# Stick-breaking attention weights by sigmoid and running product with queries on partitions, and one set of adaLN sums by ScalarE products and accumulating transfers

## The chip, the cores and the metric

The kernel runs on one core of one Trainium2 chip. The metric is the device time of one execution in microseconds, the median of several runs. A profiled execution of the kernel before took 1203.4 us; its span in the profile, from the first instruction to the last, is 1201.6 us, so 1.8 us lie around the span.

## The reference, cut to what matters

A trunk of two layers over 512 tokens of width 1024, batch 1. Layer 0 mixes tokens by stick-breaking attention (16 heads of 64), layer 1 by a gated token MLP; each is followed by a SwiGLU of width 2816, and every sub-layer takes a shift, a scale and a gate from a conditioning vector (adaLN). The two pieces that the change touches:

```python
def ada_modulation(c, w, b):
    m = jax.nn.silu(c) @ w + b
    shift, scale, gate = jnp.split(m, 3, axis=-1)
...
        before = s_idx < t_idx
        log_beta = jax.nn.log_sigmoid(z)
        log_1m = jnp.where(before, jax.nn.log_sigmoid(-z), 0.0)
        later = lax.cumsum(log_1m, axis=3, reverse=True) - log_1m
        a = jnp.where(before, jnp.exp(log_beta + later), 0.0)
        outs.append(jnp.einsum('bhts,bhsd->bhtd', a.astype(v.dtype), v[:, :, :kend]))
```

So the weight of key s for query t is sigmoid(z[t,s]) times the product of (1 - sigmoid(z[t,r])) over all keys r between s and t.

## The kernel before, in words

All matrix products are made of three float32r matmuls: each operand is split into a high part (a float32r copy) and a low part (the difference), and `mm3` adds high·high, high·low and low·high. `split` (L90) writes the high part on ScalarE (or on VectorE with `hi_dve`) and the low part on VectorE (L95).

The program goes through these stages: norm and transposes of x, V and the first Q and K (0 to 66 us of the span), the second half of V (to about 98 us), eight passes over pairs of heads (98 to 296 us; pair i holds heads 2i and 2i+1), the output projection, the first SwiGLU, the gated MLP, the second SwiGLU.

In the attention stage `pe["chain"]` ties TensorE to the order in which the code is written. The other engines' streams are put in order by the scheduler when the program is built, and each engine runs its own stream strictly in order. `filler()` is a generator of other TensorE work: for each later pair, 8 steps of three 512-column matmuls for Q and 8 for K, then the first steps of the output projection; `fill(n)` takes n steps, and `FILLS` says how many go between the parts of a pair, 16 a pair. The rest of a pair before the change:

- `scores(js)`: z of a set of key blocks, keys on partitions, queries along the free axis, for both heads. The sets are B31 (blocks 3 and 1, 512 columns), B2 (256) and B0 (512). A matmul with the constant `mask_r` adds a large negative number to masked places. Then softplus(z) by ScalarE (Abs L763, Exp L765, Ln L766) and VectorE (L767), split into `sp`.
- `weigh(js, h)`: matmuls with a constant triangle and a constant block of -1 subtract, from z in PSUM, the sums of softplus over the later keys; ScalarE takes Exp (L796), VectorE splits the weights into `ar`.
- `values(js, h)`: V times the weights, added up in one PSUM bank a head (`av`).
- `finish()`: splits the output into `o`.

`Bg("G0", "A0", "B0")` (L276, L519) is the background work of this stage: for gate, scale and shift of the first boundary it loads eight blocks of 128 x 1024 weights each through SyncE's queue into a pool of two buffers (`fwork["raw"]`), and VectorE adds block times silu(c) to a sum (`ada_stt`, L270). One `bg.step` does one block; `fill` makes one step after every third filler step. Afterwards ones-matmuls (`adaps`) add the sum over partitions.

The output projection's and the SwiGLUs' own `Bg` objects work the same way.

Of the kernel before, what the change touches and what calls it, by code (L numbers as in the profile page):

```python
# [8 lines left out]
F32 = mybir.dt.float32  # L9
# [4 lines left out]
P = 128  # L14
# [12 lines left out]
def trunk(ctx: ExitStack, tc: tile.TileContext, A: dict, out: bass.AP):  # L27
# [228 lines left out]
    cr = consts.tile([P, 5, P], F32R, name="cr")  # L256
    ident_r, tri_r, mask_r, ones_r, mones_r = [cr[:, i, :] for i in range(5)]
# [18 lines left out]
    class Bg:  # L276
# [5 lines left out]
        def __init__(self, *parts, slots=False):  # L282
            self.slots = slots

            self.parts = [
                (n, int(s), int(s) + (n != "G"), {"G": 2, "A": 1, "B": 0}[n]) for n, s in parts
            ]
            self.gen = self.run()

        def run(self):  # L290
            for name, at, s, part in self.parts:
                acc = slot(F32, name, 1, D)[:, 0, :]
                ada[name, at] = acc
                nc.gpsimd.memset(acc, 0.0)
                load(acc[0:1, :], A["adab"][s, part])
# [223 lines left out]
    bg = Bg("G0", "A0", "B0")  # L519
# [136 lines left out]
    cc = stp.tile([P, 5, P], F32, name="cc")  # L656
# [6 lines left out]
    with tc.tile_pool(name="att", bufs=1) as att, tc.tile_pool(name="att2", bufs=2) as att2:  # L663
# [46 lines left out]
        FILLS = (3, 0, 3, 0, 1, 1, 2, 2, 4, 0)  # L710
# [10 lines left out]

        def attend(i):

            ob = []
            sps, zb = {}, {}
# [10 lines left out]
            def scores(js):  # L736
# [3 lines left out]
                zs = [bank(f"z{js[0]}h0"), bank(f"z{js[0]}h1")]  # L740
                zb[js] = zs
                for j in js:
                    o, n = offs[j], T - P * j
                    ks = slice(j * P, (j + 1) * P)
# [9 lines left out]
                if len(js) == 2:  # L754
                    nd = 2 * P
                    m = cr[:, 2:3, :].to_broadcast([P, 2, P])
                for h in range(2):
                    mm(zs[h][:, :nd], ident_r, m, False, False)
                t = npool.tile([P, 2, 512], F32, tag="n", name=nm("t"))
                for h in range(2):  # L760
                    z = zs[h]
                    tn = t[:, h, :N]
                    act.activation(tn, z[:, :N], AF.Abs)  # L763
                    with tc.issue_after(table.ins):
                        act.activation(tn, tn, AF.Exp, scale=-1.0)  # L765
                    act.activation(tn, tn, AF.Ln, bias=oneb[:])  # L766
                    dve.scalar_tensor_tensor(tn, z[:, :N], 0.0, tn, ALU.max, ALU.add)  # L767
                    sp = att.tile(
# [471 lines left out]
```

## Time and profile before

| | |
|---|---|
| runs | 1202.38, 1207.81, 1210.34 us; median 1207.81 us |
| profiled execution | 1203.4 us |
| its span | 1201.6 us |
| TensorE matmul busy | 1170.4 us, 97% of the span |
| VectorE / ScalarE / GpSimd busy | 885.1 us (74%) / 623.4 us (52%) / 18.2 us (2%) |
| granted TensorE clock | 0.999 |
| eight passes over the pairs | 98.2 to 296.4 us |

How to read it: matmuls overlap, so a TensorE that is busy throughout isn't one at its peak; the length of a stretch is better read from the starts of its matmuls. A row of groups gives the mean length of one instruction. The chain of waits follows the work that ended last back to its releasers. Idle time of an engine counts only where another one waits for it.

### The profile page before, as it was taken

The page shows a single profiled execution, that of the slowest core. Times are in us where ns is not written, and L with a number is a line of the kernel's source. Part 1 is how long each engine was busy: PE and PEld are TensorE (multiplying, and loading weights), DVE is VectorE, ACT ScalarE, POOL GpSimd, SP SyncE. Part 2 cuts the span into 40 slices and gives each one's busy share as a digit, 9 for nine tenths or more (in the row PEclk, how much of TensorE's full clock was granted, in tenths as well). Part 3 has the DMA queues.
Part 4 walks back from the last instruction along what each step waited for, and adds up shares of the span by engine and source line. Part 5 has one row for each costly group of instructions (what it writes and reads, how often), then busy time and mean ns, then how long its engine had stood idle before and what let it go on. Part 6 is the DMA issues. An engine that isn't in the chain of part 4 may idle for free.

```text
span 1201.6 us, 18615 instructions
## 1 busy us (share of the span) xinstructions
PE 1170.4 (97%) x7408; PEld 1029.0 (86%) x7408; DVE 885.1 (74%) x1221; ACT 623.4 (52%) x1071; POOL 18.2 (2%) x30
## 2 busy tenths in 40 slices
PE   6898999999999999999999999999999999999998
PEld 4676778787899999999887897898999999998886
DVE  4878887776698989887768766566988888783213
ACT  6455777787565555556224553535655555572212
POOL 0100000000000000000000000000000000000000
PEclk9999999999999999999999999999999999999999
DMA  8666342120443444335888466314424444245211
GB/s 316 240 208 208 110 152 78 36 71 18 140 158 107 146 138 144 131 126 171 263 278 269 158 198 223 104 73 140 135 94 155 127 155 127 89 125 173 89 53 70
DMA packets 48635, 174.15 MB, mean 145 GB/s; under 512 B 5658, under 2 KB 5786, under 8 KB 48548
## 3 DMA queue, kind: packets, MB, share of 16 engines
q1 hardware_dynamic: 46820, 166.67, 42.6%
q0 software_dynamic: 1728, 6.29, 1.4%
q8 instruction: 58, 0.95, 0.3%
q14 instruction: 29, 0.24, 0.1%
HBM read 164.56 MB, written 8.39 MB: 144 GB/s over the span
## 4 chain that ended last, share of the span: by engine, by line
PE 74%; DVE 10%; DMA 10%; ACT 3%; issue 3%; SPq 0%; DVEq 0%; ACTq 0%
PE r L71 31%; PE y L71 19%; DMA rawada<-in_ada 6%; PE pqk L71 4%; PE gu L71 4%; PE v L71 3%; PE av L71 2%; PE u L71 2%; DVE wl L95 2%; PE z3h L71 2%; PE z0h L71 2%; DVE B L270 1%; DVE A L270 1%; ACT wh L94 1%; PE tp L79 1%
## 5 line engine op out<-in xcount | busy, mean ns | idle before, releaser
L71 PE MATMUL y<-wh,as 128*128 128x512 f32 x832 | 263.9, 395 | 0.3 <-DVE G L328 0.3
L94 ACT ACTIVATE wh<-raw 128x1024 fp32r<-128x1024 f32 x112 | 118.3, 1059 | 200.8 <-PE y L71 100.8
L95 DVE TENSOR_TENSOR wl<-raw,wh 128x1024 fp32r<-128x1024 f32 x112 | 136.5, 1221 | 109.0 <-ACT wh L94 108.9
L71 PEld LDWEIGHTS y<-wh,as 128*128 128x128 f32 x832 | 156.2, 188 | 37.2 <-DVE G L328 0.8
L71 PE MATMUL r<-Sh,wl 128*128 128x256 f32 x608 | 170.3, 280 | 0.0
L71 PE MATMUL r<-Sh,wh 128*128 128x256 f32 x608 | 170.0, 280 | 0.0
L71 PE MATMUL r<-Sl,wh 128*128 128x256 f32 x608 | 170.0, 280 | 0.0
L71 PE MATMUL y<-wl,as 128*128 128x512 f32 x416 | 164.3, 395 | 0.0
L95 DVE TENSOR_TENSOR wl<-f,wh 128x1024 fp32r<-128x1024 f32 x76 | 92.7, 1220 | 36.4 <-ACT wh L94 36.4
L94 ACT ACTIVATE wh<-f 128x1024 fp32r<-128x1024 f32 x76 | 80.7, 1061 | 71.4 <-PE r L71 64.8
L71 PEld LDWEIGHTS r<-Sh,wh 128*128 128x128 f32 x608 | 114.6, 189 | 0.0
L71 PEld LDWEIGHTS r<-Sl,wh 128*128 128x128 f32 x608 | 114.5, 188 | 0.0
L71 PEld LDWEIGHTS r<-Sh,wl 128*128 128x128 f32 x608 | 114.5, 188 | 0.0
L71 PEld LDWEIGHTS y<-wl,as 128*128 128x128 f32 x416 | 78.2, 188 | 18.0
L71 PE MATMUL r<-hTh,wh 128*128 128x256 f32 x304 | 89.0, 293 | 0.0
L71 PE MATMUL r<-hTl,wh 128*128 128x256 f32 x304 | 84.9, 280 | 0.0
L71 PE MATMUL r<-hTh,wl 128*128 128x256 f32 x304 | 80.2, 280 | 0.0
L71 PEld LDWEIGHTS r<-hTh,wh 128*128 128x128 f32 x304 | 57.2, 188 | 5.3 <-DVE gu L963 1.0
L71 PE MATMUL r<-hTh,b 128*128 128x256 f32 x304 | 60.7, 282 | 0.0
L94 ACT ACTIVATE wh<-rawx 128x1024 fp32r<-128x1024 f32 x38 | 40.4, 1062 | 35.3 <-PE r L71 30.9
L71 PEld LDWEIGHTS r<-hTl,wh 128*128 128x128 f32 x304 | 57.3, 189 | 0.1
L71 PEld LDWEIGHTS r<-hTh,wl 128*128 128x128 f32 x304 | 55.2, 188 | 0.0
(245 smaller groups left out, 2658.7 us busy)
## 6 DMA issues: line engine op xcount, KB each, us to landing
rawada<-in_ada SPq DMA_DIRECT2D x80, 512.0 KB, 4.5
raw<-in_wdown SPq DMA_DIRECT2D x44, 512.0 KB, 4.1
rawy<-in_wy SPq DMA_DIRECT2D x38, 512.0 KB, 3.6
rawx<-in_wx SPq DMA_DIRECT2D x38, 512.0 KB, 4.3
raw<-in_wqk SPq DMA_DIRECT2D x16, 512.0 KB, 3.7
ada<-in_ada0p SPq DMA_DIRECT2D x12, 512.0 KB, 8.8
raw<-in_wgu SPq DMA_DIRECT2D x12, 512.0 KB, 4.0
xd<-x POOLq DMA_DIRECT2D x12, 512.0 KB, 2.9
```

The costliest lines, as they stand in the source:

```text
L71: b = nc.tensor.matmul(o, l, r, start=start, stop=stop, skip_group_check=True)
L79: last_tp[0] = nc.tensor.transpose(o, i, ident)
L94: act.activation(hi, src, AF.Copy)
L95: dve.tensor_tensor(lo, src, hi.bitcast(F32), ALU.subtract)
L270: dve.scalar_tensor_tensor(acc, w, sc[:, kk : kk + 1], acc, ALU.mult, ALU.add)
```

## The change

1. Time is reversed outside the kernel: x goes in with its tokens in reverse order, the output is reversed back, and the gated MLP's constants are turned to match. Causal order then runs along rising indices of the free axis.
2. `scores` swaps its operands: queries on partitions, keys along the free axis. ScalarE takes Sigmoid (`be`) of each head and then 1 - `be` for both heads at once (`ga`, L791). VectorE makes the running product of `ga` along the free axis (`left`, L798, one scan for each query block and head) and multiplies it by `be` (L801). The Abs/Exp/Ln, the softplus splits and the matmuls of `weigh` go.
3. The weights now have queries on partitions, and V needs keys there: `flip` transposes them on TensorE in blocks of 128 x 128 into a PSUM bank (`tw`) and splits that into `ar`, the high part now on ScalarE. `values` multiplies V by them.
4. The order of a pair and `FILLS` are new; a pair still holds 16 filler steps.
5. `Bg` of this stage adds up its 24 blocks in another way (`transfers`): GpSimd's queue loads a block into the same two buffers, ScalarE multiplies it in place by silu(c) (L305), and GpSimd's queue sends it on with an adding transfer into the sum in SBUF (L306). Gate, scale and shift go in turn. The 24 multiply-adds of VectorE go. The other `Bg` objects stay.

The diff, cut to its core:

```diff
+        def transfers(self):
+            accs = [self.begin(*p) for p in self.parts]
+            for k in range(KD):
+                for (name, at, s, part), acc in zip(self.parts, accs):
+                    raw = fwork["raw"].tile([P, D], F32, tag="raw2", name=nm("rawada"))
+                    nc.gpsimd.dma_start(out=raw[:], in_=A["ada"][s, part, k])
+                    yield
+                    act.activation(raw[:], raw[:], AF.Copy, scale=sc[:, k : k + 1])
+                    nc.gpsimd.dma_start(out=acc, in_=raw[:], accum_op=ALU.add)
...
-    bg = Bg("G0", "A0", "B0")
+    bg = Bg("G0", "A0", "B0", summed=True)
...
-        FILLS = (3, 0, 3, 0, 1, 1, 2, 2, 4, 0)
+        FILLS = (3, 2, 3, 2, 2, 2, 2)
...
                         mm3(
-                            zs[h][:, o : o + n], kt[r, 0, ks], kt[r, 1, ks],
-                            q[r, 0, j * P : T], q[r, 1, j * P : T], j == js[0], False,
+                            z[h][:, o : o + n], q[r, 0, js_], q[r, 1, js_],
+                            kt[r, 0, j * P : T], kt[r, 1, j * P : T],
+                            j == js[0], False,
                         )
...
+                b = att.tile([P, 2, T], F32, tag="be", bufs=2, name=nm("be"))
+                g = att.tile([P, 2, T], F32, tag="ga", bufs=3, name=nm("ga"))
+                with tc.issue_after(table.ins):
+                    for h in range(2):
+                        act.activation(b[:, h, :N], z[h], AF.Sigmoid)
+                last_act[0] = act.activation(g[:, :, :N], b[:, :, :N], AF.Copy, scale=-1.0, bias=1.0)
+                e = left[nleft[0] % 2]
+                nleft[0] += 1
                 for h in range(2):
...
+                    for j in js:
+                        o, n = offs[j], T - P * j
+                        gj = g[:, h, o : o + n]
+                        dve.tensor_tensor_scan(
+                            e[:, h, o + 1 : o + n + 1], gj, gj, 1.0, ALU.mult, ALU.bypass
+                        )
+                dve.tensor_tensor(g[:, :, :N], b[:, :, :N], e[:, :, :N], ALU.mult)
...
+            def flip(blocks, h):
+                ps = bank("tw")
+                n = 0
+                for jj, js in blocks:
+                    for j in js:
+                        g, o = weights[j]
+                        o += (jj - j) * P
+                        transpose(ps[:, n : n + P], g[:, h, o : o + P])
+                        n += P
+                ar = att2.tile([P, 2, T], F32R, tag="ar", name=nm("ar"))
+                split(ar[:, 0, :n], ar[:, 1, :n], ps[:, :n])
+                turned[blocks[0][0], h] = ar
...
+        LATE = ((2, (2,)), (3, (2, 3)))
+        EARLY = ((0, (0,)), (1, (0, 1))), ((2, (0, 1)), (3, (0, 1)))
...
             scores(B0)
             fill(next(F))
-            values(B2, 0)
-            values(B2, 1)
+            flip(LATE, 0)
+            flip(LATE, 1)
+            fill(next(F))
+            values(LATE, 0, False)
+            values(LATE, 1, False)
             fill(next(F))
             if i + 1 < NPAIR:
                 cur = attend(i + 1)
                 cur[0](B31)
             fill(next(F))
-            weigh(B0, 0)
-            weigh(B0, 1)
+            for h in range(2):
+                flip(EARLY[0], h)
             fill(next(F))
+            for h in range(2):
+                values(EARLY[0], h, False)
+                flip(EARLY[1], h)
+            fill(next(F))
+            for h in range(2):
+                values(EARLY[1], h, True)
+            finish()
             if i + 1 < NPAIR:
                 cur[0](B2)
             fill(next(F))
```

Three places show how the instruction streams change. A number behind a name counts tiles.

VectorE, middle of a pair. `t` is softplus, `sp` and `ar` are low halves of splits, `wl` and `k` those of a weight and of K. Before:

```order
L95 TENSOR_TENSOR k_1466<-pqk_1341,k_1466 128x512
L95 TENSOR_TENSOR wl_1603<-raw_1600,wh_1602 128x1024
L767 SCALAR_TENSOR_TENSOR t_1482<-z0h_269_1472,t_1482 128x512
L767 SCALAR_TENSOR_TENSOR t_1482<-z0h_270_1473,t_1482 128x512
L95 TENSOR_TENSOR sp0h_272_1487<-t_1482,sp0h_272_1487 128x512
L95 TENSOR_TENSOR sp0h_273_1494<-t_1482,sp0h_273_1494 128x512
```

And now, in pair 3, from the scans of set B0 (the first row) to the splits of the first early flip:

```order
L798 SCALAR_TENSOR_TENSOR left_585<-ga_1594 128x512 x2
L95 TENSOR_TENSOR ar_1618<-tw_1614,ar_1618 128x384
L801 TENSOR_TENSOR ga_1594<-be_1593,left_585 128x1024
L95 TENSOR_TENSOR ar_1625<-tw_1621,ar_1625 128x384
L95 TENSOR_TENSOR wl_1814<-raw_1811,wh_1813 128x1024
L95 TENSOR_TENSOR k_1662<-pqk_1569,k_1662 128x512
L798 SCALAR_TENSOR_TENSOR left_584<-ga_1692 128x128
L798 SCALAR_TENSOR_TENSOR left_584<-ga_1692 128x384
L798 SCALAR_TENSOR_TENSOR left_584<-ga_1692 128x128
L798 SCALAR_TENSOR_TENSOR left_584<-ga_1692 128x384
L95 TENSOR_TENSOR ar_1711<-tw_1707,ar_1711 128x384
L801 TENSOR_TENSOR ga_1692<-be_1691,left_584 128x1024
```

The low halves of the late flips (`ar_1618`, `ar_1625`) stand behind the scans of B0, the second one also behind B0's product with `be`; those of the first early flip stand behind the four scans of the next pair's B31.

TensorE, end of K of the next pair. Before, with the last matmul of K (`pqk_1341`) in the first row:

```order
L71 MATMUL pqk_1341<-hTh_130,wl_979 128x512
L71 MATMUL z0h_269_1472<-q_1074,k_1205 128x512 x3
L71 MATMUL z0h_270_1473<-q_1074,k_1205 128x512 x3
L71 MATMUL z0h_269_1472<-cr 128x128
L71 MATMUL z0h_270_1473<-cr 128x128
L71 MATMUL pqk_1497<-hTh_124,wh_1083 128x512
L71 MATMUL pqk_1497<-hTl_125,wh_1083 128x512
L71 MATMUL pqk_1497<-hTh_124,wl_1084 128x512
L71 MATMUL av_265_1449<-ar2h_263_1438,Vh_133 128x256 x2
L71 MATMUL av_265_1449<-ar2h_263_1438,Vl_137 128x256
L71 MATMUL av_266_1456<-ar2h_264_1446,Vh_133 128x256 x2
L71 MATMUL av_266_1456<-ar2h_264_1446,Vl_137 128x256
```

Behind these rows came two more filler steps and then the scores that read the new K. Now:

```order
L71 MATMUL pqk_1095<-hTh_130,wl_798 128x512
L71 MATMUL pqk_1183<-hTh_124,wh_857 128x512
L71 MATMUL pqk_1183<-hTl_125,wh_857 128x512
L71 MATMUL pqk_1183<-hTh_124,wl_858 128x512
L71 MATMUL z3h_233_1197<-k_1180,q_1088 128x128 x3
```

One filler step stands between the last matmul of K (`pqk_1095`) and the scores that read it (`k_1180`).

ScalarE in pair 1, where the products for adaLN (`rawada`) now stand; `be` and `ga` are sigmoid and its complement, `ar` high halves, `wh` a weight's, `k` K's:

```order
L790 ACTIVATE be_1115<-z0h_215_1105 128x512
L790 ACTIVATE be_1115<-z0h_216_1106 128x512
L305 ACTIVATE rawada_1158<-rawada_1158,sc 128x1024
L791 ACTIVATE ga_1116<-be_1115 128x1024
L94 ACTIVATE ar_1140<-tw_1136 128x384
L94 ACTIVATE ar_1147<-tw_1143 128x384
L305 ACTIVATE rawada_1195<-rawada_1195,sc 128x1024
L94 ACTIVATE wh_1335<-raw_1333 128x1024
L94 ACTIVATE k_1180<-pqk_1095 128x512
L305 ACTIVATE rawada_1248<-rawada_1248,sc 128x1024
L305 ACTIVATE rawada_1289<-rawada_1289,sc 128x1024
L790 ACTIVATE be_1213<-z3h_233_1197 128x512
```

GpSimd's queue, which held no instruction in this stage before, now alternates loads and adding transfers:

```order
L303 DMA rawada_866<-in_ada 128x1024
L303 DMA rawada_897<-in_ada 128x1024
L306 DMA G_673<-rawada_866 128x1024
L306 DMA A_676<-rawada_897 128x1024
L303 DMA rawada_938<-in_ada 128x1024
L303 DMA rawada_987<-in_ada 128x1024
L306 DMA B_679<-rawada_938 128x1024
L306 DMA G_673<-rawada_987 128x1024
```

Of the 24 products on ScalarE, six stand ahead of pair 0's sigmoids of B2, six more behind these in pair 0, seven in pair 1 and five in pair 2. A load waits until the adding transfer out of the same buffer is done, a product waits for its load, and everything behind the product on ScalarE waits with it.

More of the change, by code (lines that the diff above doesn't have):

```diff
@@ L719, in fill @@
                     bg.step(1)
+        left = [att.tile([P, 2, T + 4], F32, name=nm("left")) for _ in range(2)]
+        for t in left:
+            nc.gpsimd.memset(t[:], 1.0)
+        nleft = [0]
         def attend(i):
             ob = []
-            sps, zb = {}, {}
+            weights = {}
             vc = slice(i % 4 * P, (i % 4 + 1) * P)
@@ L801, in values @@
[L801 to L814 removed]
+                    mm(z[h][:, :nd], ident_r, m, False, False)
```

131 lines of the change are left out of this document (43 added, 88 removed).

## The prediction

> **What bounds the kernel now.** I read the page's first lines, then busy times by stretch, one stretch a pair of heads, then the chain of waits inside two pairs, then the groups of VectorE and ScalarE.
>
> ```profile
> span 1201.6 us, 18615 instructions
> ...
> PE 1170.4 (97%) x7408; PEld 1029.0 (86%) x7408; DVE 885.1 (74%) x1221; ACT 623.4 (52%) x1071; POOL 18.2 (2%) x30
> ```
>
> The columns of the next rows are length, then busy time (and instructions) of TensorE, its weight loads, VectorE, ScalarE, GpSimd, then granted clock, DMA share, GB/s.
>
> ```profile
> 98.20:126.70 28.50, 24.43 (x136) 19.10 (x135) 23.88 (x34) 17.48 (x34) 0.00 (x0) 1.00 0.58 185
> 126.70:151.40 24.70, 24.70 (x140) 19.69 (x139) 20.37 (x34) 18.05 (x36) 0.00 (x0) 1.00 0.37 109
> 151.40:177.40 26.00, 24.87 (x140) 19.68 (x139) 22.46 (x35) 17.96 (x36) 0.00 (x0) 1.00 0.49 159
> 177.40:201.80 24.40, 24.40 (x141) 19.97 (x140) 18.76 (x34) 19.06 (x38) 0.00 (x0) 1.00 0.21 65
> 201.80:229.40 27.60, 26.14 (x146) 20.81 (x145) 21.04 (x37) 20.36 (x41) 0.00 (x0) 1.00 0.17 58
> 229.40:254.50 25.10, 25.10 (x144) 20.51 (x144) 17.69 (x31) 20.14 (x40) 0.00 (x0) 1.00 0.14 43
> 254.50:278.30 23.80, 23.64 (x136) 19.21 (x135) 15.68 (x29) 17.04 (x35) 0.00 (x0) 1.00 0.26 89
> 278.30:296.40 18.10, 18.08 (x96) 13.86 (x95) 11.43 (x23) 11.94 (x22) 0.00 (x0) 1.00 0.00 0
> ```
>
> The full pairs take 24 to 28 us, and TensorE is busy nearly throughout at full clock (the first pair apart), while VectorE is idle for 4 to 8 us of each and ScalarE for 5 to 11. In this stage TensorE sets the time; other engines matter only when they make it wait. The chain says what its 24 us hold:
>
> ```profile
> 172.29 2.79 PE pqk L71 x12
> 175.08 0.93 PE z2h L71 x8
> 176.01 1.55 PE av L71 x6
> ...
> 179.66 1.84 PE z3h L71 x12
> ...
> 183.60 0.86 PE z2h L71 x8
> 184.46 1.78 PE av L71 x12
> ...
> 186.94 1.27 PE z0h L71 x8
> ...
> 188.94 0.72 PE av L71 x6
> ...
> 191.05 1.50 PE z3h L71 x14
> ...
> 194.40 2.56 PE z0h L71 x16
> ```
>
> A filler step is three of the `pqk` matmuls, 2.79 / 4 = 0.70 us, and 16 of them make 11.2. Scores with masks are 1.27 + 1.50 + 0.93 = 3.70, `weigh` is 1.84 + 0.86 + 2.56 = 5.26, `values` 1.78 + 0.72 + 1.55 = 4.05. Sum 24.2, against stretches of 24.4 and 24.7: before the change nearly nothing waits.
>
> **The change part by part: TensorE's work.** `weigh` goes: -5.26 us a pair. Scores keep their shapes. The transposes are 20 a pair (10 for each head):
>
> ```profile
> 344.81 1.09 PE L79 MATMUL tp<-identt,t 128*128 128x128 f32 x8 [0.34 <-DVE t L387]
> 345.65 0.37 PE L71 MATMUL gu<-hTl,wh 128*128 128x256 f32 x1
> ```
>
> Eight of the same type start within 345.65 - 344.81 = 0.84 us, 0.105 each, so +2.10. `values` keeps its columns but cuts them into twelve 128-wide and twenty-four 256-wide matmuls. The 256-wide cost 0.72 / 6 = 0.12 above, the 128-wide 0.10:
>
> ```profile
> 185.21 0.33 PE L71 MATMUL av<-ar3h,Vh 128*128 128x128 f32 x2
> 185.38 0.27 PE L71 MATMUL av<-ar3h,Vl 128*128 128x128 f32 x1
> 185.50 0.40 PE L71 MATMUL av<-ar3h,Vh 128*128 128x384 f32 x1
> ```
>
> (three between 185.21 and 185.50). That is 4.1 us, as before. TensorE's work falls by 3.15 us to 21.0 us a pair, 25 us in all. Were that the whole story, the time would be 1178.
>
> **New waits in a pair.** Here are the rows that price the new chain of ScalarE and VectorE.
>
> ```profile
> L95 DVE TENSOR_TENSOR wl<-raw,wh 128x1024 fp32r<-128x1024 f32 x27 | 33.0, 1221 | 13.1 <-ACT wh L94 13.1
> L95 DVE TENSOR_TENSOR ar3h<-a,ar3h 128x512 fp32r<-128x512 f32 x16 | 11.0, 690 | 0.4
> ...
> L767 DVE SCALAR_TENSOR_TENSOR t<-z0h,t 128x512 f32<-128x512 f32 x16 | 10.3, 687 | 7.8 <-ACT t L766 7.8
> ...
> L270 DVE SCALAR_TENSOR_TENSOR A<-rawada,sc,A 128x1024 f32<-128x1024 f32 x8 | 10.3, 1282 | 3.2 <-DMA rawada<-in_ada 3.2
> ...
> L95 DVE TENSOR_TENSOR ar2h<-a,ar2h 128x256 fp32r<-128x256 f32 x16 | 6.8, 425 | 0.5
> ```
>
> ```profile
> L94 ACT ACTIVATE wh<-raw 128x1024 fp32r<-128x1024 f32 x26 | 27.5, 1058 | 31.8 <-PE pqk L71 16.1 <-DMA raw<-in_wqk 4.5 <-PE y L71 4.2
> ...
> L763 ACT ACTIVATE t<-z0h 128x512 f32<-128x512 f32 x16 | 8.7, 596 | 3.0 <-PE z0h L71 3.0
> ```
>
> Sigmoid I price like the 512-wide ScalarE row (0.6, two in 1.1 us), the complement and each product for adaLN like the 1024-wide one (1.06), the product of `be` and `left` like `wl` (1.22), the low half of a 384-wide flip between 0.43 and 0.69, at 0.55. No row shows a scan. It can't be quicker than a plain pass over 512 columns, 0.69 us; and since each column needs the product of the one before, which none of these rows does, I take two passes, the time of 1024 plain columns less a little, 1.2 us (upper end 1.28). [...]
>
> Now I walk through an undisturbed pair, from the start of its scores of B0, with 0.1 us for a hand-over (my allowance). TensorE by itself reaches the late `values` after 1.27 + 3 steps 2.1 + late flips 0.63 + 2 steps 1.4 = 5.4 us. ScalarE has a copy of Q and a `wh` ahead, so the sigmoids run from 1.7 to 2.8 and the complement to 3.9. On VectorE the low halves of the late flips stand behind both scans: these end at 6.3, the first half at 6.9, the product with `be` at 8.1, the second half at 8.7. So the late `values` end at 9.4 instead of 6.8: 2.5 us lost (1.4 with a plain scan). Next, K's last matmul is now one step (0.70 us) ahead of the scores that read it, which must let ScalarE copy (0.6) and VectorE subtract (0.69): 0.9 us lost. Then the scores of B31 end, and until the early `values` TensorE has 2 + 2 steps and flips, 3.4 us; in their way stand two sigmoids 1.1, complement 1.06, four scans 2.5 and a low half 0.55, in all 5.4 with hand-overs, and the second head waits for the 1.22 us product as well: 2.5 us lost (1.6 with a plain scan). The other waits (B2's weights, the last flips) have their fillers. The pair comes to 21.0 + 5.9 = 27 us (25 with a plain scan). In order of code nothing else can fill these gaps on TensorE.
>
> Pairs 3 to 6 took 24.4 + 27.6 + 25.1 + 23.8 = 100.9; four of 27 and the 2.8 us of `adaps` (12 matmuls like the `pqk` ones) are 110.8: **+10 us**. The last pair has TensorE's output projection to fill gaps and keeps most of its 3.15: **-2**.
>
> **The adaLN sums.** What leaves VectorE (24 times 1.28) was no bound and earns nothing by itself. What comes is a chain with two buffers: load, product, adding transfer, load again.
>
> ```profile
> rawada<-in_ada SPq DMA_DIRECT2D x80, 512.0 KB, 4.5
> ...
> xd<-x POOLq DMA_DIRECT2D x12, 512.0 KB, 2.9
> ```
>
> ```profile
> q0 software_dynamic: 1728, 6.29, 1.4%
> ```
>
> ```profile
> DMA to landing us min/median/max: 3.5/4.4/4.9
> ```
>
> The last row is the loads of this stage; I take 3.8 for one from GpSimd's queue. No row shows an adding transfer. Its floor is the plain transfer of that queue and size, 2.9. It must fetch the old sum as well: the 12 `xd` transfers took 1.4% of 1201.6 = 16.8 us of all engines, 1.4 us each, and once more of that makes 4.3, which I take; as upper end I set three plain transfers, 8.7 (two fetches and a store each as long as one). A buffer's round is then 3.8 + 1.06 + 4.3 + 0.5 for issue and hand-overs = 9.7 us, a product each 4.85 us, while ScalarE's stream has seven in pair 1, 34 us, and five in pair 2. Behind each stand sigmoids and splits that TensorE waits for. Counting from the seventh product, which I put at pair 0's start of 98.2 or a little later (99), 17 more rounds end at 99 + 17 * 4.85 = 181.5; after the last product pair 2 still has its last splits, `values`, scores of B2 and fillers, 10 us. So pair 2 ends at 191.5 instead of 177.4: **+14 us**. With 2.9 for the adding transfer and 3.5 for the load a product comes each 4.0 us, the pairs' own 27 us decide, and it is about +4; with 8.7 each 7.05 us: 99 + 120 + 10 = 229, +52.
>
> **Sum.** 14 + 10 - 2 = +22 on the profiled execution's 1203.4: 1225. This execution lies 4.4 us below the median of the runs, 1207.8, on which the same sum gives 1230; between the two I say **1227 us**. The first stage and all behind the attention keep their streams.
>
> **The rivals.**
> - *TensorE keeps what it saves* (faster). The place is VectorE's stream: if scans cost at most a plain pass and ScalarE's pieces overlap more than I let them, the loss in a pair falls from 5.9 to about 2.2, and transfers like `xd` don't hold up pairs 0 to 2. Pairs 3 to 6 then take 4 * 23.2 + 2.8 = 95.6 (-5), pairs 0 to 2 lose 6, the last 3: 1189. For it: VectorE idles a quarter of a pair now. Against it: its order is fixed. The point that decides is a loss of 3.15 us a pair.
> - *Gains and waits cancel.* Plain scans (25 us a pair, +2 for pairs 3 to 6), adding transfers as quick as `xd` (+1), last pair -2: 1204.
> - *Slow adding transfers.* At 8.7 us: 1203 + 52 + 10 - 2 = 1263.
>
> That the change doesn't do what it says I leave out: the streams show the new operations and none of the old.
>
> **How the numbers follow.** The forecast has 0.46 (own range 1213 to 1245), faster 0.16, cancel 0.26, slow transfers 0.12. A measurement of this kernel tells about 1% from no change, that is 1196 to 1220. Nearly all of the first rival is below it, cancel and the forecast's low tail within: faster 0.15, same 0.28, slower 0.57. The range 1190 to 1262 leaves half of the first and of the last rival out.
>
> **What would show it.** In the profile after: L798 on 512 columns near 1.2 us and not 0.69; pairs 3 to 6 near 27 us, with TensorE waiting for VectorE's `ar` and for `k`; in pairs 0 to 2 ScalarE waiting for `rawada` by 20 us or more, adding transfers landing after some 4.3 us. It is wrong if ScalarE doesn't wait for `rawada`, or if TensorE's waits in a later pair stay under 3 us.

## The result, and the profile after

| | before | after |
|---|---|---|
| median | 1205.71 us (1202.38 to 1210.34) | 1275.61 us (1272.85 to 1278.41) |
| profiled execution / its span | 1203.4 / 1201.6 us | 1276.3 / 1273.8 us |
| granted TensorE clock | 0.999 | 0.970 |

The changed kernel is slower: ratio 1.0577, interval 1.0531 to 1.0623, +70 us. The forecast was 1227 with a range up to 1262. The side was right, the size was not. The page of the profile after:

```profile
span 1273.8 us, 18377 instructions
...
PE 1183.0 (93%) x7376; PEld 1036.4 (81%) x7376; DVE 858.1 (67%) x1141; ACT 599.4 (47%) x975; POOL 54.3 (4%) x80
...
PE   7995756879899999999999999999999999999998
...
PEclk9997788999989999999999999999999999999999
```

TensorE's busy time *grew* by 13 us although, by the prediction's working, 25 us of its work are gone: in slices 4 to 7 (95 to 223 us) it has gaps, and its clock is 0.7 to 0.8 there. The stretches by pair, each from the first B0 score matmul of a pair to that of the next, columns as in the prediction (the last three are granted clock, DMA share, GB/s):

```profile
101.65:147.36 45.71, 31.86 (x134) 24.46 (x135) 20.30 (x27) 22.37 (x33) 10.09 (x15) 0.74 0.78 192
147.36:194.77 47.41, 28.01 (x136) 21.59 (x135) 17.16 (x24) 20.23 (x30) 9.99 (x14) 0.82 0.73 179
194.77:232.59 37.82, 26.55 (x135) 21.04 (x134) 17.84 (x25) 18.28 (x28) 6.59 (x9) 0.86 0.77 194
232.59:260.23 27.64, 23.01 (x138) 18.30 (x137) 18.18 (x26) 13.16 (x23) 0.00 (x0) 1.00 0.23 82
260.23:291.94 31.71, 25.14 (x141) 20.14 (x141) 20.84 (x30) 14.30 (x25) 0.00 (x0) 0.95 0.10 34
291.94:319.57 27.63, 24.82 (x140) 19.85 (x139) 17.67 (x25) 14.36 (x25) 0.00 (x0) 0.94 0.13 39
319.57:346.51 26.94, 23.43 (x133) 18.59 (x132) 16.97 (x23) 11.96 (x21) 0.00 (x0) 0.94 0.23 79
346.51:364.02 17.51, 14.36 (x75) 11.73 (x75) 9.62 (x13) 7.52 (x12) 0.00 (x0) 0.81 0.00 1
```

So the 72.2 us between the spans lie here: pair 2 ends at 232.59 instead of 177.4 (**+55.2**; forecast +14), pairs 3 to 6 take 113.9 instead of 100.9 (**+13.0**; forecast +10), the last pair 17.5 instead of 18.1 (-0.6; forecast -2), and what comes behind takes 1273.8 - 364.02 = 909.8 instead of 905.2 (+4.6; forecast 0). Nearly the whole miss, 41 of 50 us, is in pairs 0 to 2. Who waits there (98 to 233 us; total, times, longest):

```profile
ACT rawada L305 <- DMA rawada<-in_ada: 60.6, 14, 8.9
DVE left L798 <- ACT ga L791: 32.8, 9, 11.5
PEld av L71 <- ACT ar L94: 23.7, 7, 8.2
POOL B L306 <- ACT rawada L305: 23.0, 6, 7.2
PE av L71 <- ACT ar L94: 20.8, 6, 7.7
```

ScalarE stands 60.6 us in front of products whose block has not landed; behind it stand the sigmoids (VectorE waits for `ga`) and the high halves `ar` (TensorE waits for them). The products themselves:

```profile
61.20 2.42 ACT L305 ACTIVATE rawada<-rawada,sc 128x1024 f32<-128x1024 f32 x2 [0.65 <-DMA rawada<-in_ada]
...
112.33 1.15 ACT L305 ACTIVATE rawada<-rawada,sc 128x1024 f32<-128x1024 f32 x1 [6.54 <-DMA rawada<-in_ada]
...
223.87 1.15 ACT L305 ACTIVATE rawada<-rawada,sc 128x1024 f32<-128x1024 f32 x1 [3.06 <-DMA rawada<-in_ada]
```

The row at 112.33 is the seventh product, the last row the 24th: 17 products in 111.5 us, 6.56 us each (the chain's pace, below), where the forecast had a start at 99 and 4.85. Of the 41 us, the start makes 13.3, the pace 17 x 1.71 = 29.1, and what follows the last product -1.3 (8.7 us, not 10). The prices of a round of the loop, as transfers (count, KB, median us from issue to landing):

```profile
rawada<-in_ada POOLq DMA_DIRECT2D x24, 512.0 KB, 5.4
G<-rawada POOLq DMA_DIRECT2D x8, 512.0 KB, 4.9
A<-rawada POOLq DMA_DIRECT2D x8, 512.0 KB, 6.5
B<-rawada POOLq DMA_DIRECT2D x8, 512.0 KB, 5.0
```

and as instructions that issue them on GpSimd (busy time, mean ns):

```profile
L303 POOL DMA_DIRECT2D rawada<-in_ada x24 | 13.3, 555 | 56.3 <-DMA G<-rawada 23.9 <-DMA A<-rawada 16.4 <-DMA B<-rawada 15.7
L306 POOL DMA_DIRECT2D A<-rawada x8 | 7.4, 923 | 16.2 <-ACT rawada L305 16.1
L306 POOL DMA_DIRECT2D G<-rawada x8 | 7.1, 884 | 34.7 <-ACT rawada L305 20.7 <-DMA A<-in_adab 14.1
```

Load 5.4, product 1.15, adding transfer 5.0 (into G and B; into A it takes 6.5), its issue 0.88 and the load's 0.55 are 13.0 us for a round of two buffers, or 13.5 with the mean of the three transfers. That is 6.5 to 6.7 us a product, what the rows at ScalarE show. The start is explained by one more row of GpSimd and by SP's queue:

```profile
73.56 0.89 POOL L306 DMA_DIRECT2D G<-rawada  x1 [14.06 <-DMA A<-in_adab]
```

```profile
52.21 9.94 SPq L88 DMA_DIRECT2D raw<-in_wv  x3
69.24 0.33 SPq L88 DMA_DIRECT2D raw<-in_wqk  x1
69.66 0.31 SPq L88 DMA_DIRECT2D G<-in_adab  x1
```

The first two products were done at 63.6, but an adding transfer may not go before the 4 KB row `adab` has landed in the sum's first partition, and these rows stand on SP's queue behind weight loads: the first adding transfer goes 10 us after its product.

The new VectorE work costs what was forecast:

```profile
L798 DVE TENSOR_TENSOR_SCAN left<-ga 128x512 f32<-128x512 f32 x16 | 18.7, 1211 | 8.6 <-ACT ga L791 8.6
L798 DVE TENSOR_TENSOR_SCAN left<-ga 128x384 f32<-128x384 f32 x16 | 14.9, 933 | 0.0
```

### The profile page after: what moved, and what is told of

Same layout as the page of the kernel before. It is cut to its first block, busy times and chain, and to the rows that moved or that the text cites. A ratio compares the mean times of both kernels' runs of the same rounds, so it can differ in the third digit from the quotient of the medians.

```text
span 1273.8 us, 18377 instructions
## 1 busy us (share of the span) xinstructions
PE 1183.0 (93%) x7376; PEld 1036.4 (81%) x7376; DVE 858.1 (67%) x1141; ACT 599.4 (47%) x975; POOL 54.3 (4%) x80
## 4 chain that ended last, share of the span: by engine, by line
PE 57%; DVE 7%; DMA 7%; ACT 2%; issue 1%; DVEq 0%; ACTq 0%
PE r L71 29%; PE y L71 18%; DMA rawada<-in_ada 3%; PE gu L71 3%; DVE wl L95 2%; PE u L71 2%; PE v L71 2%; DMA raw<-in_wdown 1%; DMA raw<-in_win_v 1%; ACT wh L94 1%; PE sv L71 1%; DVE B L270 1%; PE av L71 1%; DMA raw<-in_wgu 1%; DVE x L396 1%
## 5 line engine op out<-in xcount | busy, mean ns | idle before, releaser
L71 PEld LDWEIGHTS y<-wl,as 128*128 128x128 f32 x416 | 78.4, 189 | 18.1
L71 PE MATMUL av<-ar,Vh 128*128 128x128 f32 (+1 forms) x192 | 50.1, 330 | 43.9 <-DVE ar L95 22.8
L798 DVE TENSOR_TENSOR_SCAN left<-ga 128x128 f32<-128x128 f32 (+2 forms) x64 | 48.4, 809 | 52.1 <-ACT ga L791 52.0
L71 PEld LDWEIGHTS av<-ar,Vh 128*128 128x128 f32 x192 | 36.8, 218 | 54.8 <-DVE ar L95 29.1
L305 ACT ACTIVATE rawada<-rawada,sc 128x1024 f32<-128x1024 f32 x24 | 27.6, 1149 | 74.7 <-DMA rawada<-in_ada 69.5
```

What stands on the lines that cost most here:

```text
L71: b = nc.tensor.matmul(o, l, r, start=start, stop=stop, skip_group_check=True)
L305: act.activation(raw[:], raw[:], AF.Copy, scale=sc[:, k : k + 1])
L798: dve.tensor_tensor_scan(e[:, h, o + 1 : o + n + 1], gj, gj, 1.0, ALU.mult, ALU.bypass)
```

## The experiments

Every ratio below is to the kernel before, run on the same chip beside it, with its 95% interval.

### The two halves of the change

**The attention alone**, with the sums as before:

```diff
-    bg = Bg("G0", "A0", "B0", summed=True)
+    bg = Bg("G0", "A0", "B0")
```

> The changed kernel with the new attention, but the adaLN sums as before: loads by SP's queue, the multiply-add on VectorE. Theory (the chain of adding transfers holds up pairs 0 to 2, the attention costs about what was forecast): pairs 3 to 6 stay near 28 us each, pairs 0 to 2 fall from 131 us to about 85 to 95, and the time to 1225 us (1213 to 1237). Rival (the new order of the attention itself, or the lower clock that comes with its waits, costs the bulk): pairs 0 to 2 stay above 115 us and the time at 1255 or more.

1231.3 us, ratio 1.0204 (1.0163 to 1.0245). Its stretches of pairs 0 to 2:

```profile
98.33:128.48 30.15, 25.91 (x136) 20.34 (x135) 26.06 (x32) 13.22 (x23) 0.00 (x0) 0.89 0.55 173
128.48:160.83 32.35, 25.96 (x135) 20.36 (x134) 24.19 (x29) 12.64 (x22) 0.00 (x0) 0.89 0.42 131
160.83:191.14 30.31, 24.29 (x135) 19.06 (x134) 20.84 (x27) 12.64 (x22) 0.00 (x0) 0.94 0.37 122
```

92.8 us instead of the 130.9 of the changed kernel; pairs 3 to 6 take 116.4. So without the chain 44 of the 70 us are gone. But +25 us remain, where the forecast had +8 for the attention, or about +12 with the +4 that it named for pairs 0 to 2 when the pairs' own length decides there. (The profile is of this kernel's longest execution, 1235.9 us, 4.5 above its median, so its stretches are a little long.)

**The sums alone**, in the kernel before (`transfers`, `begin` and `summed=True` put into it, nothing else):

> The kernel before with the adaLN sums by ScalarE products and adding transfers alone; its attention is untouched. Theory: the chain load, product, adding transfer sets pairs 0 to 2 by itself, pair 2 ends near 225 us instead of 177, time 1250 us (1235 to 1262). Rival (products are late because the new attention's ScalarE work and waits hold them up): pair 2 ends before 195 us and the time is below 1225.

1258.3 us, ratio 1.0432 (1.0390 to 1.0475): +52 by the chain alone, with the old attention. Its seventh product starts at 114.1 and its last at 227.2, 6.65 us for each of the 17 between: the same pace with quite another ScalarE stream, so the chain sets it. The halves add up to 77 us, the change has 70; the likely reason, which no run separates, is that in pairs 0 to 2 the attention's waits lie partly inside the chain's.

### Inside the chain

**Rows early.** Only the start is touched:

```diff
-            load(acc[0:1, :], A["adab"][s, part])
+            if self.summed:
+                nc.gpsimd.dma_start(out=acc[0:1, :], in_=A["adab"][s, part])
+            else:
+                load(acc[0:1, :], A["adab"][s, part])
```

> The changed kernel; only the three 4 KB rows adab are loaded on GpSimd's queue, straight behind the memsets, not on SP's queue behind the weight loads. Theory: the first adding transfers go out about 10 us earlier, the seventh product comes near 100 us instead of 112, and the whole chain ends 10 to 13 us earlier: 1264 us (1259 to 1270). Rival (the start does not matter, since pace or the other waits decide): 1272 or more.

1268.9 us, ratio 1.0523 (1.0485 to 1.0561), against 1.0577: the medians lie 6.7 us apart, though the two intervals overlap. The seventh product came at 105.9, 6.4 us earlier (10 to 13 were expected), and the pace stayed at 6.5. The first adding transfer went out at 61.37 instead of 73.56, but the third product came at 78.81 instead of 84.69, only half as much earlier. On ScalarE's in-order stream splits that wait for weight loads now stood ahead of it:

```profile
71.55 1.06 ACT L94 ACTIVATE wh<-raw 128x1024 fp32r<-128x1024 f32 x1 [5.13 <-DMA raw<-in_wqk]
74.70 1.06 ACT L94 ACTIVATE wh<-raw 128x1024 fp32r<-128x1024 f32 x1 [2.09 <-DMA raw<-in_wqk]
...
78.81 2.18 ACT L308 ACTIVATE rawada<-rawada,sc 128x1024 f32<-128x1024 f32 x2
```

So the late start is in part the 4 KB rows and in part this order and the slow rounds before the seventh product.

**Plain transfers** in place of the adding ones:

```diff
-                    nc.gpsimd.dma_start(out=acc, in_=raw[:], accum_op=ALU.add)
+                    nc.gpsimd.dma_start(out=acc, in_=raw[:])
```

> The changed kernel with plain transfers of the same size from rawada to G, A and B in place of the adding ones, so the adaLN sums are left out of what it computes. Theory (fetching the old sum is what makes an adding transfer dear; a plain one lands after 2.9 us like xd): the pace of the chain falls from 6.6 to about 5 us a product, pairs 0 to 2 from 131 to about 103 us, time 1249 us (1240 to 1260). Rival (a copy from SBUF to SBUF on GpSimd's queue is as slow without the adding): plain transfers land after 4.5 us or more and the time is 1268 or more.

1249.4 us, ratio 1.0361 (1.0313 to 1.0408). The same rows of this run:

```profile
G<-rawada POOLq DMA_DIRECT2D x8, 512.0 KB, 3.0
A<-rawada POOLq DMA_DIRECT2D x8, 512.0 KB, 4.4
B<-rawada POOLq DMA_DIRECT2D x8, 512.0 KB, 2.9
```

The adding costs 2 us of landing (4.9, 6.5, 5.0 against 3.0, 4.4, 2.9) and 0.35 us of issue (0.88 against 0.53). The pace fell to 5.43 us and the seventh product came at 100.9.

**Loads by SP**, so that GpSimd's queue holds only the adding transfers:

```diff
-                    nc.gpsimd.dma_start(out=raw[:], in_=A["ada"][s, part, k])
+                    load(raw[:], A["ada"][s, part, k])
```

> The changed kernel with the loads of rawada on SP's queue again, the adding transfers alone on GpSimd's. Theory (loads land after about 4 us there instead of 5.4, and GpSimd's queue holds transfers alone): pace about 5.8 us a product, time 1262 us (1255 to 1269). Rival (on SP's queue the loads wait for their buffer and hold the weight loads behind them): weights come late in pairs 0 to 2 and the time is 1275 or more.

1262.1 us, ratio 1.0464 (1.0432 to 1.0496), the expected time: pace 6.07 (about 5.8 expected), start 103.4. The loads did not land after about 4 us: the 80 `rawada` loads of the whole run, all on SP's queue here, have a median of 4.9; on GpSimd's queue the 24 of the chain have 5.4 in the changed kernel and 4.6 in the run with the sums alone. So the queue is not shown to be what made the load dear. The weight loads `raw<-in_wqk`, on SP's queue in both kernels, went from 3.7 to 4.9 us with the change, and to 4.8 with the sums alone: loads land later beside the chain's traffic.

With this run the DMA engines' own cost can be told apart. GpSimd's queue took 9.6% of 1273.8 us, 122.3 us of all 16 engines, in the changed kernel; 6.8% of 1256.7, 85.5, here, where the 24 loads are elsewhere; and 7.2% of 1240.6, 89.3, with plain transfers. Without the 16.8 us of `xd`, an adding transfer takes (85.5 - 16.8) / 24 = 2.9 us, a load (122.3 - 85.5) / 24 = 1.5, and a plain one (89.3 - 16.8 - 36.8) / 24 = 1.5. So the adding makes up 1.4 of the 2.9 us, about what a plain transfer takes in all.

**Four buffers** in place of two:

```diff
-                    raw = fwork["raw"].tile([P, D], F32, tag="raw2", name=nm("rawada"))
+                    fwork["two"].append(fwork["two"].pop(0))
+                    pool, tag = fwork["two"][0]
+                    raw = pool.tile([P, D], F32, tag=tag, bufs=2, name=nm("rawada"))
...
+        fwork["two"] = [(fwork["raw"], "raw2"), (att, "raw3")]
...
-                b = att.tile([P, 2, T], F32, tag="be", bufs=2, name=nm("be"))
+                b = npool.tile([P, 2, T], F32, tag="n", name=nm("be"))
```

> The changed kernel with four rawada buffers in place of two (the be tiles go to another pool of two buffers of the same size to make room). Theory (the pace of 6.6 us a product is one round of load, product and adding transfer shared by two buffers): the pace falls to about 4.4 us, what the DMA engines need, pairs 0 to 2 to 95 to 105 us, time 1243 us (1230 to 1256). Rival (the DMA engines or the single GpSimd queue set the pace already): pace stays above 6 us and time above 1267.

1259.8 us, ratio 1.0445 (1.0401 to 1.0489): between theory and rival. Its first two pairs:

```profile
101.91:153.52 51.61, 34.28 (x134) 25.95 (x134) 21.63 (x30) 27.40 (x39) 15.36 (x22) 0.70 0.95 234
153.52:187.43 33.91, 27.51 (x136) 21.43 (x135) 16.66 (x23) 18.26 (x28) 6.95 (x9) 0.83 0.91 243
```

The DMA share is 0.95 and 0.91: the round is shared by four buffers now, but the engines are nearly full, loads land after 8.4 us instead of 5.4, and the pace ends at 5.24. The chain has a second floor right under the first: 2.9 + 1.5 = 4.4 us of all engines for a product, beside the other loads.

### Inside the attention

All of these stand on the run with the attention alone (1231.3 us).

**A plain pass for the scan:**

```diff
-                        dve.tensor_tensor_scan(
-                            e[:, h, o + 1 : o + n + 1], gj, gj, 1.0, ALU.mult, ALU.bypass
-                        )
+                        dve.tensor_tensor(e[:, h, o + 1 : o + n + 1], gj, gj, ALU.mult)
```

> The new attention with the adaLN sums as before, each running product replaced by a plain elementwise pass over the same columns, so the running product is left out of what it computes. Theory (scans at two passes cost 2 us of TensorE's time a pair, 27 against 25 us): eight pairs lose 2 us less, time 1216 us (1210 to 1223) against 1231. Rival (the price of the scan hides behind other waits): 1227 or more.

1211.1 us, ratio 1.0048 (1.0033 to 1.0062). What a scan takes beyond a plain pass (1211 ns for 512 columns against the 690 of the 512-wide `ar3h` row in the prediction) costs 19 us by the ratios, a little more than the 16 expected here, and every one of the eight pairs is shorter than in the run with the attention alone, by 2 to 5 us: it lies on the path in every pair.

**Another order of code:** late flips ahead of the scores of B0, both early flips ahead of the next scores of B31, four `ar` buffers (the `be` tiles go to another pool to make room), `FIRST = (3, 8)`:

```diff
-            scores(B0)
-            fill(next(F))
-            flip(LATE, 0)
-            flip(LATE, 1)
+            for h in range(2):
+                flip(LATE, h)
+            scores(B0)
             fill(next(F))
...
+            for h in range(2):
+                flip(EARLY[1], h)
+            for h in range(2):
+                values(EARLY[0], h, False)
             if i + 1 < NPAIR:
                 cur = attend(i + 1)
                 cur[0](B31)
...
-        FILLS = (3, 2, 3, 2, 2, 2, 2)
+        FILLS = (3, 4, 1, 1, 2, 5)
```

> The new attention with the adaLN sums as before (the base is the kernel of the run with the attention alone, 1231 us), in another order of code: the late flips stand ahead of the scores of B0, both early flips ahead of the next pair's scores of B31, so that on VectorE the low halves come ahead of the next scans; K's last matmul is three filler steps ahead of its scores. Theory (the lost 5.9 us a pair are VectorE's and ScalarE's in-order queues, nothing else): pairs 3 to 6 fall from 116 to about 92 us, pairs 0 to 2 to about 80 to 85, time 1198 us (1188 to 1212). Rival (the work of the new attention itself or the lower granted clock sets the pairs): pairs 3 to 6 stay above 108 us and the time above 1220.

1215.0 us, ratio 1.0082 (1.0055 to 1.0110): half of the expected gain, between theory and rival. Pairs 0 to 2 fell to 80.2 us, pairs 3 to 6 only to 108.2. The waits of TensorE for `ar` are gone but for one of 0.8 us, and it now waits for the weights `ga` themselves before the late flips, up to 4.8 us (3.1 in pairs 3 to 6), and at the adaLN broadcasts, 2.1 and 2.7 us.

**K two steps earlier**, `FIRST` alone:

```diff
-        FIRST = (3, 6)
+        FIRST = (3, 8)
```

The place in the run with the attention alone, first as TensorE's rows, then as two windows (clock third from the end):

```profile
173.11 0.40 PE L71 MATMUL pqk<-hTh,wl 128*128 128x512 f32 x1
174.20 0.32 PE L71 MATMUL z3h<-k,q 64*128 64x128 f32 x1 [0.70 <-ACT k L94]
175.58 1.86 PE L71 MATMUL z3h<-k,q 64*128 64x128 f32 x11 [1.06 <-DVE k L95]
```

```profile
173.50:175.58 2.08, 0.33 (x2) 0.18 (x1) 1.83 (x2) 0.65 (x2) 0.00 (x0) 1.00 0.87 297
175.58:179.10 3.52, 3.52 (x16) 2.89 (x17) 0.00 (x0) 1.08 (x2) 0.00 (x0) 0.52 0.86 298
```

Why so long, ScalarE's and VectorE's rows of the same time tell:

```profile
172.61 1.06 ACT L94 ACTIVATE wh<-raw 128x1024 fp32r<-128x1024 f32 x1 [5.95 <-PE pqk L71]
173.57 0.58 ACT L94 ACTIVATE k<-pqk 128x512 fp32r<-128x512 f32 x1
```

```profile
173.70 1.23 DVE L95 TENSOR_TENSOR wl<-raw,wh 128x1024 fp32r<-128x1024 f32 x1 [0.67 <-ACT wh L94]
174.84 0.68 DVE L95 TENSOR_TENSOR k<-pqk,k 128x512 fp32r<-128x512 f32 x1
```

K's last matmuls release the weight buffer too, and on both queues the split of the next weight block stands ahead of K's own.

> The new attention with the adaLN sums as before (1231 us), with two more filler steps ahead of the first pair, so that in every pair K's last matmul is three filler steps ahead of the scores of B31 that read it, not one; nothing else differs. In the run with the attention alone TensorE stands 2.07 us at this place (173.51 to 175.58, one matmul between), and the next 3.52 us run at a granted clock of 0.52. Theory (this wait and the half clock behind it are on the path of every pair): seven pairs lose 1.4 us of waiting and some 1 to 1.7 us of slow clock less, time 1212 us (1206 to 1220). Rival (VectorE's queue sets the pairs, and the time only moves to the waits for ar and ga): 1225 or more.

1223.5 us, ratio 1.0160 (1.0123 to 1.0197): a gain of 5 us by the ratios and 8 by the medians, outside the theory's range and 1.5 us under the rival's mark. The waits for K are gone from the list, but those for `ar` grew. The row of the run with the attention alone, then of this one, from 98 to 330 us:

```profile
PE av L71 <- DVE ar L95: 19.1, 24, 2.7
```

```profile
PE av L71 <- DVE ar L95: 26.8, 26, 3.2
```

**Useless matmuls in the gaps**, to hold the clock up:

```diff
+        def spin(o, n, start):
+            for _ in range(n):
+                mm(o, zero[:], hTk(hT, 0, 0, o.shape[-1])[0], start, False)
...
                     ob.append(bank(f"av{h}"))
+                    spin(ob[h][:], 6 * (h == 0), True)
+                elif h == 0 and not stop:
+                    spin(ob[0][:, 256:512], 12, False)
```

> The new attention with the adaLN sums as before (1231 us), and TensorE is given useless matmuls with a zero operand, in place of standing still, ahead of the first late values (6 of 512 columns) and ahead of the first early values (12 of 256 columns), 2.8 us a pair in all. Theory (a gap of TensorE of about 2 us or more is followed by 3.4 us at half the granted clock, and this is a part of what the attention costs): the granted clock in pairs 3 to 6 goes from 0.88 to 0.94 up to 0.98 or more, and the time falls by 6 to 16 us, to 1220 us (1214 to 1226), though TensorE has more to do. Rival (the waits of VectorE's and ScalarE's queues set the pairs whatever the clock): 1230 or more, since the added matmuls only stand in the way.

1228.7 us, ratio 1.0197 (1.0166 to 1.0227): no difference that can be told. The clock did come back, to 1.00 in four of the eight pairs (0.81 to 0.94 before). Neither number was met. The added matmuls take 2.8 us a pair, 22 in all, while the waits for `ar` fell by 13 us only (19.1 to 6.4), so they partly stand ahead of work that was ready. Nor is every gap of about 2 us followed by the slow clock, as the theory has it (see the last section). The run shows that holding the clock this way earns nothing; what the lower clock alone costs stays open.

**Without most multiply-adds:**

```diff
-                    ada_stt(acc, raw, k)
+                    if self is not bg or k == 0:
+                        ada_stt(acc, raw, k)
```

> The new attention with the adaLN sums as before (1231 us), but only the first of the eight multiply-adds of each sum is made, so most of the adaLN sums is left out of what it computes; the loads stay. Theory (with scans on VectorE the 24 multiply-adds of 1.28 us are on the path in pairs 0 to 2, where they were free before): pairs 0 to 2 fall from 93 to about 82 us, pairs 3 to 6 stay at 116, time 1220 us (1214 to 1225). Rival (pairs 0 to 2 are set by the weights' loads or TensorE's waits elsewhere): pairs 0 to 2 stay above 89 us, time 1227 or more.

1232.5 us, ratio 1.0215 (1.0177 to 1.0252): no change in the time, the rival's number, though not by the rival's mechanism. In its profile pairs 0 to 2 did fall, from 92.8 to 85.0 us, part of the theory's gain, but pairs 3 to 6 took 119.2 instead of 116.4 and the later stages 2.5 more. Why these moved was not tried, and the two profiles are of executions that lie 4.5 us above and 2.7 us below their medians; what the multiply-adds cost in pairs 0 to 2 stays open.

### Can a version beat both?

All of these are the reordered attention with the sums as loads by SP.

**ScalarE empties the broadcast's bank**, and the broadcast comes a step later (`act.activation(acc[:, c], ps[:], AF.Copy, bias=...)`, then a VectorE product in SBUF):

> The reordered attention (1215 us), where TensorE's longest waits in pairs 3 to 6 are at the adaLN broadcasts: adaps matmuls waiting for their low half on VectorE (2.1 us) and the projection waiting for the bank that VectorE still has to empty (2.7 us). Here ScalarE empties that bank, VectorE multiplies in SBUF behind it, and the broadcast comes one step of the background work later. Theory: these waits and the half clock behind them go, pairs 3 to 6 from 108 to about 100 us, time 1208 us (1203 to 1212). Rival (the waits only move to other places, since VectorE's queue holds everything): 1213 or more.

1212.0 us, ratio 1.0051 (1.0030 to 1.0073), at the upper end of the theory's range; the interval overlaps that of the reordered attention (1.0055 to 1.0110), so the gain is hardly told from noise. Pairs 3 to 6 fell from 108.2 to 104.2 us (100 expected); the waits partly moved, as the rival has it.

**The same with the sums' additions on GpSimd:**

```diff
-                    ada_stt(acc, raw, k)
+                    act.activation(raw, raw, AF.Copy, scale=sc[:, k : k + 1])
+                    nc.gpsimd.tensor_tensor(acc, acc, raw, ALU.add)
```

> The kernel of the run before with the adaLN multiply-adds as ScalarE products and additions on GpSimd, the loads on SP's queue as in the kernel before the change. Theory (in pairs 0 to 2 VectorE's multiply-adds, 24 of 1.28 us, set the reordered attention): pairs 0 to 2 fall from 80 to about 70 us, time 1199 us (1192 to 1206), below the kernel before. Rival (an addition on GpSimd takes over 3 us or slows VectorE, and the products hold up ScalarE's queue as in the changed kernel): pairs 0 to 2 above 85 us, time 1215 or more.

1234.9 us, ratio 1.0251 (1.0224 to 1.0277): the rival, with pairs 0 to 2 at 97.1 us. An addition takes 2.6 us (not over 3), VectorE's pass `wl` over 128x1024 took 1.48 us in pair 0 instead of 1.21 (the run before), ScalarE again waits 17.7 us for blocks, and GpSimd waits for the `adab` rows as in the changed kernel:

```profile
L323 POOL TENSOR_TENSOR G<-G,rawada 128x1024 f32<-128x1024 f32 x8 | 21.0, 2622 | 25.9 <-DMA G<-in_adab 15.1 <-ACT rawada L322 10.6
```

**The scores of B2 straight behind the early values** (`FILLS = (3, 4, 1, 1, 7)`), the broadcast's low halves on GpSimd:

> The reordered attention (1215 us; 1212 with the adaLN broadcasts a step later), in which TensorE waits for the weights of B2 before the late flips, up to 4.8 us: the scores of B2 come straight behind the early values, so their chain on ScalarE and VectorE has seven filler steps instead of five; ScalarE empties the broadcast's bank and GpSimd makes its low halves. Theory: the waits before the late flips and before adaps go, time 1201 us (1194 to 1208). Rival (VectorE's amount of work, 25 us in pairs 0 and 2, sets these pairs, and the order is nothing to it): 1209 or more.

1210.5 us, ratio 1.0039 (1.0018 to 1.0059): the rival's time, and not told from the 1212.0 of two runs above. TensorE still waits for `ga` before the late flips, up to 3.6 us, and at a broadcast, 3.2 us.

**And the sums spread**, `ADA_AT = 4`:

> The kernel of the run before with a step of the adaLN sums every fourth filler step instead of every third, so that VectorE's multiply-adds are spread over more pairs. If VectorE's amount of work sets pairs 0 to 2, these fall by 4 to 8 us and the time is 3 to 8 us below that of the run before (1196 us, 1189 to 1204); if the order and the waits set them, it is the same within 2 us, or longer, since the last broadcasts come late.

1206.5 us, ratio 0.9999 (0.9978 to 1.0020). The gain of 4 us has the expected size, but its place is another: pairs 0 to 2 took 76.2 us instead of 77.8, not 4 to 8 us less, pairs 3 and 4 took 47.4 instead of 52.9, and pair 6 took 32.3, with the last broadcasts in it. The 1196 us were reckoned from the 1201 expected of the run before.

**Spread, then dense** (every fourth filler step up to the eightieth, then every third):

> The reordered attention with the scores of B2 early and the multiply-adds spread (1206.5 us), whose sixth pair took 32.3 us because the last adaLN broadcasts came there together: a step of the adaLN sums every fourth filler step up to the eightieth, then every third, so that the broadcasts are spread over the pairs behind. Theory: that pair falls to about 26 us and the time to 1201 us (1196 to 1206), under the kernel before. Rival (the broadcasts cost the same wherever they stand): 1205 or more.

1205.0 us, ratio 0.9996 (0.9974 to 1.0018), inside the theory's range and at the rival's mark. Level with the kernel before, not below it: pair 6 fell to 25.3 us, but pair 5 now takes 30, with a broadcast that waits 4.2 us behind VectorE's queue. No version here beats the kernel before; order, spreading and the broadcast's moved work win back the attention's 25 us, no more.

## Why the prediction was right in sign and wrong in size

- **The mis-sized term is the adaLN chain**, +14 against +55 for the end of pair 2. The two-buffer round was the right mechanism, and the run with the sums alone shows it. Its sizes were not: the load stood at 3.8, for which no reason is given beside the prediction's own row with a median of 4.4 (it is 5.4 here); the adding transfer at 4.3 (4.9 to 6.5); the product at 1.06 (1.15); "0.5 for issue and hand-overs" is less than the two issues alone (0.88 + 0.55). Each is a little short; in a loop of 17 products, at 6.56 us each for 4.85, they make 29 us. The rows for these prices came from a kernel without this traffic.
- **"Counting from the seventh product, which I put at ... 99"** had no row under it; it came at 112.3. The step left out a queue: the transfers were traced on GpSimd's, but their first one waits for a row of 4 KB on SP's. Moving the rows brought the start 6.4 us forward, half of the 13.3.
- **Adding costs a second transfer's time:** "once more of that" was right, 2.9 against 1.5 us of the engines, as the queue shares show; that this time is the fetch of the old sum was the author's reasoning, and no run shows it. The rival with 8.7 us came nearest to the time (1263 for 1275.6), but by luck: its adding transfers were too long, its load and issues too short and its start too early.
- **The scan at two passes** was the author's estimate, with no row of a scan under it; the length was right (1211 ns for 512 columns, forecast 1.2), and so was its place on the path: the plain pass won 19 us.
- **Pairs 3 to 6** came out at 113.9 for 110.8. TensorE's waits there in the changed kernel:

```profile
PE av L71 <- DVE ar L95: 10.2, 12, 2.7
PE z3h L71 <- DVE k L95: 3.2, 3, 1.1
PE z3h L71 <- ACT k L94: 2.1, 3, 0.7
PE adaps L71 <- DVE k L95: 2.1, 1, 2.1
```

These are 17.6 us in four pairs, where the forecast had 4 x 5.9 = 23.6. Before the late `values` TensorE waits 1.1 to 2.7 us (2.5 forecast), before the early ones 0 to 1.8 (2.5). K's wait is 1.8 (0.9), because the walk left out the weight block's split that stands ahead of K's on both engines. In pair 5 the waits add up to 2.8 us, under the 3 us that the prediction gave as a sign of being wrong. What the sum had not at all is the clock: 0.94 to 0.95 in three of the four. Shorter waits and a term left out work against each other, so that the total came so close is partly luck.
- **Attention in pairs 0 to 2:** the sum let the chain set them and put the attention's own loss there at nothing. Run alone it loses 13.6 us there in its profile; the halves and the whole (77 and 70 us) let some 7 us of the attention's cost be hidden behind the chain, by the totals alone.
- **"All behind the attention keep their streams"**: 4.6 us more in the profile. The stages behind took 907 to 913 us in the runs with the new attention, but also 907.2 in the run with the sums alone, whose attention is the old one, against 905.2 in the profile before. So the new attention is not shown to be the reason; the cause stays open.

## What to carry to other kernels

A sum moved from VectorE to adding transfers is not free: each round passes through a load, an engine, an issue and a transfer that took the DMA engines twice a plain one's time here (2.9 against 1.5 us), and the engine that makes the product then waits in order with everything behind it. Price such a loop by all its steps, with landing times as they are beside the traffic that it adds, and divide by the buffers; then look whether the DMA engines are the next floor. And before a transfer's start is set down, follow *every* operand that it waits for to its own queue, the small ones too.

## What the runs showed of the hardware

- A short stand of TensorE can be followed by a lower clock. In the kernel before, with no wait of TensorE above 1.55 us in this stage, the clock is 1.00 in all eight pairs; in the run with the attention alone, behind 2.07 us with one matmul in them, it was 0.52 for 3.52 us. But the length of the stand doesn't settle it: in the run with another order of code 2.08 us (up to 214.09) were followed by a clock of 0.51 for 3.38 us, where matmuls of 512 columns start 0.42 us apart; in the changed kernel 2.08 us (up to 276.21) were followed by a clock of 1.00 over the next 3.40 us. Behind 2.25 us (up to 150.48) in the run with another order of code, and behind 3.31 us (up to 166.28) in the run with the additions on GpSimd, these matmuls start 0.23 us apart, as they did ahead of the wait. What decides stays open, and so does what the slow stretch costs: the run with useless matmuls got some of the clock back and no time.
- A 512 KB transfer within SBUF by GpSimd's queue lands after 2.9 to 4.4 us (medians by target, two buffers), an adding one after 4.9 to 6.5, and issuing it takes 0.88 instead of 0.53 us.
- GpSimd's addition of 128x1024 fp32 takes 2.6 us, and VectorE's 128x1024 pass `wl` took 1.48 us in pair 0 beside such additions, 1.21 without.
